# Attention logits of a two-layer trunk: one float32 product, or three float32r products of high and low parts

## The chip, the core and the metric

The kernel runs on one core of a Trainium2 chip. The metric is the device time of one execution in microseconds (us). Data passes between the engines of the core by semaphores: TensorE (PE, matmuls and transposes into PSUM), VectorE (DVE), ScalarE (ACT), GpSimd (POOL) and SyncE (SP, which here issues DMAs). Each engine works through its own instructions in order.

## The reference

The input is 512 tokens of 1024 features. Layer 0 is a Mamba-2 mixer and a convolutional feed-forward block (FFN). Then keys and values are projected once from the stream, and layer 1 is a differential attention over them and a second FFN. The change is in the attention, which is, cut to what matters:

```python
q = rms_norm((rms_norm(x, ln_g) @ q_w).reshape(b, s, 8, 2, 64), q_norm_g)   # k alike
logits = einsum('bqhcd,bkhcd->bhcqk', qblk, k) * 64 ** -0.5 + bias
p = softmax(where(dist >= 0, logits, -inf))
attn = p[:, :, 0] - lam * p[:, :, 1]
o = einsum('bhqk,bkhd->bqhd', attn, v)
```

There are 8 heads. Each has two maps c, each with a query and a key vector of 64 elements; the two softmax maps are subtracted with a learned weight, and the difference is applied to one value vector of 128 elements. The result of each head is normalised and goes through the output projection. Everything is float32.

## The kernel before

The kernel keeps the stream transposed: `xT` is 8 tiles of 128 features by 512 tokens. Large matmuls aren't done in float32. Both operands are split into a high part, rounded to float32r, and a low part, the float32r difference, and `mm3` (lines 174 to 177) adds three float32r products: high by high, high by low, low by high. Weights are loaded in an order fixed by `plan` (lines 68 to 116), two chunks ahead of their use, by SP (line 138), and split on arrival by ScalarE (lines 144, 148) and VectorE (lines 145, 149).

The attention begins at line 761. `proj` (line 783) makes 512 columns of a projection for all tokens: four chunks of weights, and for each 24 float32r matmuls 512 columns wide into four PSUM banks (lines 791 to 793), 96 in all. `qk` (line 805) does that for the keys or queries of four heads (k0 and q0 are heads 0 to 3, k1 and q1 heads 4 to 7). Its evacuation scales each 128 tokens by ScalarE (line 811), squares (812) and sums by VectorE (813). After an inverse square root (`rsqrt_act`, line 336) VectorE normalises (820), TensorE transposes (824), and ScalarE copies to SBUF with the gain (825). The tiles `kT[i]` and `qT[i]` (lines 779, 780) are [128, 4, 512], float32: the 128 rows of a head are map 0 on rows 0 to 63 and map 1 on rows 64 to 127. `vproj` (829) does the values.

A head is three units (`Unit`, line 837): query blocks 0 and 1 together, block 2, and block 3, of 128 queries each, which see 128, 256, 384 and 512 keys. A unit goes through four steps. `logits` (847): for each block and each map, one float32 matmul of 64 rows (line 867), in PSUM bank m for map m; VectorE adds the bias and takes the maximum (870); ScalarE does the exponentials with their sums (878). `weigh` (881): the reciprocal and the subtraction of the maps (883 to 888). `turn` (891): transposes (896) and a copy by ScalarE (897). `values` (899): float32 matmuls with the values (905) and a copy (908). After the last unit of a head `finish` (911) normalises its output, transposes it (921) and splits it (924, 925). The bias of a head is loaded as a Toeplitz tile `tr` from a small table in DRAM (852) and reversed by VectorE (853).

`heads` (929) staggers the steps of successive units. `weave` (368) puts pieces of other work between them: with heads 0 to 3 stand the projections k1, q1 and v1, with heads 4 to 7 the output projection of heads 0 to 3 (`attn_out`, line 952, 96 matmuls); the output projection of heads 4 to 7 comes last. On top of that a scheduler sets the final order of each engine's instructions, and moves some of them past others. The buffers come from pools: of a tag with n buffers, the tile after n others reuses the first, once that is no longer read.

```python
for m in range(2):
    rows = slice(64 * m, 64 * (m + 1))
    pe.matmul(pss[m][:, c], qT[i2][rows, h4, i * P:(i + 1) * P], kT[i2][rows, h4, :n],
              start=True, stop=True)
```

Of the kernel before, what the change touches and what calls it, by code (L numbers as in the profile page):

```python
# [9 lines left out]
F32 = mybir.dt.float32  # L10
F32R = mybir.dt.float32r
I32 = mybir.dt.int32
AF = mybir.ActivationFunctionType
ALU = mybir.AluOpType
# [4 lines left out]
P = 128  # L19
T = 512  # L20
D = 1024
KB = D // P
NT = T // P
# [8 lines left out]
AH = 8  # L32
# [7 lines left out]
def trunk_kernel(ctx: ExitStack, tc, x, ssm_ln_g, ssm_in_w, ssm_conv_w, ssm_conv_b, ssm_dt_bias,  # L40
# [62 lines left out]
    def tok_plan(key, w, c0, gcol):  # L103
        for k in range(0, KB, 2):
            plan.append(("%s_%d" % (key, k), *w_cols(w, k, 2, c0, 512), gcol + k))
# [2 lines left out]
    tok_plan("q0", q_w[0], 0, 40)  # L108
    tok_plan("v0", kv_w, D, 32)
    tok_plan("k1", kv_w, 512, 32)  # L110
    tok_plan("q1", q_w[0], 512, 40)
    tok_plan("v1", kv_w, D + 512, 32)
    for i in range(2):
        for c in range(4):
            plan.append(("ao%d_%d" % (i, c), *w_cols(attn_out_w[0], 4 * i, 4, c * 256, 256)))
# [84 lines left out]
    c2 = cp.tile([P, 80], F32, name="c2")  # L200
# [16 lines left out]
    with tc.tile_pool(name="ph0", bufs=1) as p0:  # L217
# [43 lines left out]
        ps = aux_bank("pst")  # L261
# [74 lines left out]
    def rsqrt_act(v, pl, name, shape, n):  # L336

        m = pl.tile(shape, F32, tag="rs_m", name="rsm_" + name, bufs=2)
        t = pl.tile(shape, F32, tag="rs_t", name="rst_" + name, bufs=2)
        dve.tensor_scalar(out=m, in0=v, scalar1=1.0 / n, scalar2=EPS, op0=ALU.mult, op1=ALU.add)  # L340
        act.activation(v, m, AF.Ln)
        act.activation(v, v, AF.Exp, scale=-0.5)
        dve.tensor_tensor(out=t, in0=v, in1=v, op=ALU.mult)
        dve.scalar_tensor_tensor(out=t, in0=t, scalar=-0.5, in1=m, op0=ALU.mult, op1=ALU.mult)
        dve.scalar_tensor_tensor(out=v, in0=t, scalar=1.5, in1=v, op0=ALU.add, op1=ALU.mult)
# [18 lines left out]
    def run(gen):  # L364
        for _ in gen:
            pass
# [11 lines left out]
    def chain(*gens):  # L378
        for g in gens:
            yield from g  # L380
# [380 lines left out]
    with tc.tile_pool(name="att_o", bufs=1) as op_, tc.tile_pool(name="att", bufs=1) as ap:  # L761
# [5 lines left out]
        hb = NBIAS // 2  # L767
        for i in range(2):
            oh = ap.tile([32, hb], F32, tag="p0", name="oh%d" % i, bufs=3)
            bv = ap.tile([AH, hb], F32, tag="p1", name="bv%d" % i, bufs=3)  # L770
            sync.dma_start(oh, onehot[:, i * hb:(i + 1) * hb])
            ps = aux_bank("ps_rb%d" % i)
            pe.matmul(ps[:AH, :hb], rb, oh, start=True, stop=True)
            act.activation(bv, ps[:AH, :hb], AF.Copy)
            if i == 0:
                dve.memset(bv[:, 0:P - 1], NEG)
            sync.dma_start(bd[:, i * hb:(i + 1) * hb], bv)

        kT = [ap.tile([P, 4, T], F32, name="kT%d" % i) for i in range(2)]
        qT = [ap.tile([P, 4, T], F32, name="qT%d" % i) for i in range(2)]  # L780
        vt = [ap.tile([P, D], F32, name="vt%d" % b) for b in range(NT)]

        def proj(key, evac):
# [19 lines left out]
            yield  # L803

        def qk(key, dst, gcol):
            kn, ss = [], ap.tile([P, NT, 8], F32, tag="qss", name="ss" + key, bufs=2)

            def evac(b, ps, rt):
                t = ap.tile([P, T], F32, tag="kn", name="kn%s_%d" % (key, b), bufs=4)
                s = ap.tile([P, T], F32, tag="ksq", name="ksq%s_%d" % (key, b), bufs=1)  # L810
                act.activation(t, ps, AF.Copy, scale=rt[:, 2 * b:2 * b + 1])
                act.activation(s, t, AF.Square)
                dve.reduce_sum(ss[:, b, :], s.rearrange("p (a q) -> p a q", a=8), axis=AX.X)
                kn.append(t)

            yield from proj(key, evac)
            rsqrt_act(ss, ap, key, [P, NT, 8], 64)
            for b in range(NT):
                v = kn[b].rearrange("p (a q) -> p a q", a=8)
                dve.tensor_tensor(out=v, in0=v, in1=ss[:, b, :].unsqueeze(2).to_broadcast([P, 8, 64]),  # L820
                                  op=ALU.mult)
                ps = aux_bank("kt%s_%d" % (key, b))
                for h in range(4):
                    pe.transpose(ps[:, h * P:(h + 1) * P], kn[b][:, h * P:(h + 1) * P], ident)
                act.activation(dst[:, :, b * P:(b + 1) * P], ps.rearrange("p (h t) -> p h t", h=4),
                               AF.Copy, scale=c2[:, gcol:gcol + 1])
            yield

        def vproj(key, i):
            def evac(b, ps, rt):  # L830
                act.activation(vt[b][:, i * 512:(i + 1) * 512], ps, AF.Copy, scale=rt[:, 2 * b:2 * b + 1])
            yield from proj(key, evac)
# [4 lines left out]
        class Unit:  # L837
# [9 lines left out]
            def logits(self):  # L847
                h, tag, st = self.h, self.tag, self.st
                if self.part == 0:
                    st["tb"] = ap.tile([P, T], F32, tag="tb", name="tb%d" % h, bufs=2)  # L850
                    tr = ap.tile([P, T], F32, tag="tr", name="tr%d" % h, bufs=1)
                    sync.dma_start(tr, bass.AP(tensor=bd.tensor, offset=h * NBIAS, ap=[[1, P], [1, T]]))
                    dve.tensor_copy(st["tb"], tr[:, ::-1])
                    st["ot"] = ap.tile([P, NT, P], F32, tag="ot", name="ot%d" % h, bufs=2)
                i2, h4 = h // 4, h % 4
                k = len(self.ii)
                mx = ap.tile([P, k, 2], F32, tag="mx%d" % k, name="mx" + tag, bufs=3)
                self.sm = ap.tile([P, k, 2], F32, tag="sm%d" % k, name="sm" + tag, bufs=3)
                self.p = [ap.tile([P, T], F32, tag="p%d" % m, name="lg%s_%d" % (tag, m), bufs=3)
                          for m in range(2)]  # L860
                pss = [aux_bank("lg%s_%d" % (tag, m)) for m in range(2)]
                for j, i in enumerate(self.ii):
                    n = (i + 1) * P
                    c = slice(self.off[j], self.off[j] + n)
                    for m in range(2):
                        rows = slice(64 * m, 64 * (m + 1))
                        pe.matmul(pss[m][:, c], qT[i2][rows, h4, i * P:(i + 1) * P], kT[i2][rows, h4, :n],
                                  start=True, stop=True)
                    for m in range(2):
                        dve.tensor_tensor_reduce(self.p[m][:, c], pss[m][:, c],  # L870
                                                 st["tb"][:, (3 - i) * P:], 1.0, -3.0e38,
                                                 ALU.add, ALU.max, mx[:, j, m:m + 1])
                dve.tensor_scalar(out=mx, in0=mx, scalar1=-1.0, scalar2=None, op0=ALU.mult)
                for j, i in enumerate(self.ii):
                    n = (i + 1) * P
                    for m in range(2):
                        v = self.p[m][:, self.off[j]:self.off[j] + n]
                        act.activation(v, v, AF.Exp, bias=mx[:, j, m:m + 1],
                                       accum_out=self.sm[:, j, m:m + 1])
# [30 lines left out]

        def finish(h, st):
            ot = st["ot"]
            sq = ap.tile([P, T], F32, tag="ksq", name="osq%d" % h, bufs=1)
            so = ap.tile([P, NT], F32, tag="so", name="so%d" % h, bufs=2)
            act.activation(sq, fl(ot), AF.Square)
            dve.reduce_sum(so, sq.rearrange("p (a q) -> p a q", a=NT), axis=AX.X)
            rsqrt_act(so, ap, "o%d" % h, [P, NT], P)
            dve.tensor_tensor(out=ot, in0=ot, in1=so.unsqueeze(2).to_broadcast([P, NT, P]), op=ALU.mult)
            ps = aux_bank("oT%d" % h)
            for i in range(NT):  # L920
                pe.transpose(ps[:, i * P:(i + 1) * P], ot[:, i, :], ident)
            oh_ = op_.tile([P, T], F32R, tag="oh", name="oh%d" % h, bufs=6)
            ol_ = op_.tile([P, T], F32R, tag="ol", name="ol%d" % h, bufs=6)
            act.activation(oh_, ps, AF.Copy, scale=c2[:, 50:51])
            dve.scalar_tensor_tensor(out=ol_, in0=ps, scalar=c2[:, 50:51], in1=oh_.bitcast(F32),
                                     op0=ALU.mult, op1=ALU.subtract)
            return oh_, ol_
# [24 lines left out]
        def attn_out(i, os, norm):  # L952
            for c in range(4):
# [7 lines left out]
                    add_to_stream(m, ps, 24, norm)  # L961
                    yield

        run(qk("k0", kT[0], 48))
        run(qk("q0", qT[0], 49))
        run(vproj("v0", 0))
        os0, os1 = [], []
        weave(heads(range(0, 4), os0),
              chain(qk("k1", kT[1], 48), qk("q1", qT[1], 49), vproj("v1", 1)), 2, 5)
        weave(heads(range(4, 8), os1), attn_out(0, os0, None), 1, 6)  # L970
        run(attn_out(1, os1, norm1))

# [37 lines left out]
```

## Time and profile before

| what | us |
|---|---|
| median of 3 runs (lowest, highest) | 1390.85 (1390.69, 1392.38) |
| the profiled execution's own time | 1389.46 |
| its span, first to last instruction | 1387.6 |
| TensorE busy | 1367.3 |
| VectorE busy | 893.6 |
| ScalarE busy | 671.5 |
| the first logits matmul starts at | 833.4 |
| the last head's transposes start at | 998.8 |

The profile is of one execution. Its views used below are the page (busy time of each engine, the span in 40 slices, the chain that ended last); the busy time of each engine in chosen stretches, where the number behind x counts instructions; the timeline of an engine (start and duration in us, line, operation, output <- inputs, shape, and how many records in a row are drawn together); the chain of work that ended last, piece by piece in order of time; and the groups of instructions by line and shape (busy us, mean ns, idle before). TensorE's matmuls are pipelined, so a record is longer than its share of the engine: what a matmul costs in a row of them is read from one start to the next. A float32 matmul leaves two records.

### The profile page before, as it was taken

To read this page: it belongs to the slowest core of one execution; us is meant where nothing else is said; L and a number is where in the kernel's file an instruction comes from. 1 tells how busy PE (TensorE), PEld (TensorE's weight loads), DVE (VectorE), ACT (ScalarE), POOL (GpSimd) and SP (SyncE) were. 2 spreads that over 40 slices of the span, in tenths; PEclk is the share of its full clock that TensorE was granted. 3 is DMA by queue.
4 is the path that set the end of the run, shared out by engine and by line. 5 is a ranking of instruction groups with operands and counts; after the bars stand their busy time and mean duration, and the time that the engine had idled before them with its cause. 6 is when DMAs were issued, how large, how long until landed. Compare 5 with 4: busy or idle time off the path is not lost.

```text
span 1387.6 us, 17001 instructions
## 1 busy us (share of the span) xinstructions
PE 1367.3 (99%) x6480; PEld 1105.0 (80%) x6480; DVE 893.6 (64%) x1481; ACT 671.5 (48%) x1108; POOL 93.2 (7%) x117
## 2 busy tenths in 40 slices
PE   8999999999999999999999999999999999999998
PEld 6777787787878888888888786786778888888886
DVE  6687767768677775357754546748687774367741
ACT  6785644742344443134433557757654442144431
POOL 4330300300020000000001000000020000000000
PEclk9999999999999999999999999999999999999999
DMA  6655433432223333233323422221133332333322
GB/s 183 163 148 148 129 91 107 129 103 65 80 88 107 91 97 101 91 104 95 93 82 112 114 90 68 66 87 39 48 103 93 93 105 91 99 99 91 99 92 69
DMA packets 188422, 137.18 MB, mean 99 GB/s; under 512 B 6852, under 2 KB 177268, under 8 KB 188340
## 3 DMA queue, kind: packets, MB, share of 16 engines
q1 hardware_dynamic: 181312, 122.93, 30.1%
q0 software_dynamic: 4400, 12.01, 2.9%
q10 hardware_dynamic: 2628, 1.15, 0.3%
q8 instruction: 51, 0.84, 0.2%
q14 instruction: 31, 0.25, 0.1%
HBM read 133.82 MB, written 2.25 MB: 98 GB/s over the span
## 4 chain that ended last, share of the span: by engine, by line
PE 76%; DVE 5%; ACT 4%; issue 1%; DMA 0%; POOL 0%; POOLq 0%; ACTq 0%
PE ps_u L175 6%; PE ps_u L177 6%; PE ps_d L176 6%; PE ps_d L177 6%; PE ps_u L176 6%; PE ps_d L175 6%; PE ps_g L176 6%; PE ps_g L177 6%; PE ps_g L175 5%; PE ps_in L175 2%; PE ps_in L177 2%; PE ps_in L176 2%; PE ps_o L176 2%; PE ps_o L177 2%; PE ps_o L175 1%
## 5 line engine op out<-in xcount | busy, mean ns | idle before, releaser
L176 PE MATMUL ps_g<-xgl,wh_g 128*128 128x512 f32 x352 | 137.2, 390 | 1.5 <-DVE xgl L319 1.5
L175 PE MATMUL ps_d<-hh,wh_d 128*128 128x512 f32 x352 | 137.5, 391 | 0.0
L177 PE MATMUL ps_d<-hh,wl_d 128*128 128x512 f32 x352 | 137.2, 390 | 0.0
L175 PE MATMUL ps_u<-xgh,wh_u 128*128 128x512 f32 x352 | 137.1, 390 | 0.0
L176 PE MATMUL ps_u<-xgl,wh_u 128*128 128x512 f32 x352 | 137.1, 390 | 0.0
L175 PE MATMUL ps_g<-xgh,wh_g 128*128 128x512 f32 x352 | 137.0, 389 | 0.1
L176 PE MATMUL ps_d<-hl,wh_d 128*128 128x512 f32 x352 | 137.0, 389 | 0.0
L177 PE MATMUL ps_u<-xgh,wl_u 128*128 128x512 f32 x352 | 136.9, 389 | 0.0
L177 PE MATMUL ps_g<-xgh,wl_g 128*128 128x512 f32 x352 | 136.9, 389 | 0.0
L175 PE MATMUL ps_in<-xgh,wh_in 128*128 128x512 f32 x320 | 126.9, 397 | 0.0
L177 PE MATMUL ps_in<-xgh,wl_in 128*128 128x512 f32 x320 | 126.3, 395 | 0.0
L176 PE MATMUL ps_in<-xgl,wh_in 128*128 128x512 f32 x320 | 125.9, 393 | 0.0
L149 DVE TENSOR_TENSOR wl_d<-wr_d,wh_d 128x1024 fp32r<-128x1024 f32 (+1 forms) x48 | 54.5, 1136 | 91.7 <-ACT wh_d L148 91.5
L148 ACT ACTIVATE wh_d<-wr_d 128x1024 fp32r<-128x1024 f32 (+1 forms) x48 | 47.5, 990 | 129.5 <-PE ps_d L176 115.3
L724 ACT ACTIVATE hh<-vg 128x512 fp32r<-128x512 f32 x44 | 27.8, 631 | 114.9 <-DVE vg L723 114.9
L707 DVE TENSOR_TENSOR uu<-ps_u,nr_f 128x512 f32<-128x512 f32 x44 | 30.4, 692 | 79.6 <-PE ps_u L177 79.6
L176 PEld LDWEIGHTS ps_g<-xgl,wh_g 128*128 128x128 f32 x352 | 66.1, 188 | 16.0 <-DVE xgl L319 2.3
L175 PEld LDWEIGHTS ps_g<-xgh,wh_g 128*128 128x128 f32 x352 | 66.1, 188 | 14.2 <-ACT xgh L318 0.5
L177 PEld LDWEIGHTS ps_u<-xgh,wl_u 128*128 128x128 f32 x352 | 66.1, 188 | 13.7
L176 PEld LDWEIGHTS ps_u<-xgl,wh_u 128*128 128x128 f32 x352 | 66.1, 188 | 13.7
L176 PEld LDWEIGHTS ps_d<-hl,wh_d 128*128 128x128 f32 x352 | 66.1, 188 | 13.6
L177 PEld LDWEIGHTS ps_d<-hh,wl_d 128*128 128x128 f32 x352 | 66.1, 188 | 13.5
(315 smaller groups left out, 2950.4 us busy)
## 6 DMA issues: line engine op xcount, KB each, us to landing
wr_g<-in_ffn_up_w_dram SPq DMA_DIRECT2D x44, 512.0 KB, 3.8
wr_u<-in_ffn_up_w_dram SPq DMA_DIRECT2D x44, 512.0 KB, 3.9
wr_in<-in_ssm_in_w_dram SPq DMA_DIRECT2D x40, 512.0 KB, 3.9
wr_d<-in_ffn_down_w_dram SPq DMA_DIRECT2D x40, 512.0 KB, 3.5
m<-cumd POOLq DMA_DIRECT2D x16, 512.0 KB, 5.1
wr_out<-in_ssm_out_w_dram SPq DMA_DIRECT2D x16, 512.0 KB, 3.4
wr_k<-in_kv_w_dram SPq DMA_DIRECT2D x8, 512.0 KB, 3.9
wr_q<-in_q_w_dram SPq DMA_DIRECT2D x8, 512.0 KB, 4.1
```

Source lines behind the costliest of these rows:

```text
L148: act.activation(wh[:, :n], raw[:, :n], AF.Copy)
L149: dve.tensor_tensor(out=wl[:, :n], in0=raw[:, :n], in1=wh[:, :n].bitcast(F32), op=ALU.subtract)
L175: pe.matmul(ps, wh, xh, start=start, stop=False)
L176: pe.matmul(ps, wh, xl, start=False, stop=False)
L177: pe.matmul(ps, wl, xh, start=False, stop=stop)
L707: dve.tensor_tensor(out=u, in0=ps, in1=r, op=ALU.mult)
L724: act.activation(h, ga, AF.Copy)
```

## The change

The transposed keys and queries are stored as a high and a low float32r part, in tiles of two heads ([128, 2, 512]) in place of four: ScalarE copies with the gain to the high part, VectorE computes the low part from the same PSUM bank. The tiles come from rings, three buffers for keys and two for queries (each for high and low). The logits of a block are three float32r products (high by high, high by low, low by high), each for both maps in turn, map 0 on rows 0 to 63 and map 1 on rows 64 to 127; they add up in PSUM. To make room, map 1 of the logits (`p1`) has two buffers for three, the squares `ksq` and `osq` and the bias tile `tr` go to tiles of the pool `bp` that the norms also use (`tr` then has two buffers), and `qss` has one buffer for two. The projection v1 moves ahead of q1, in the weights' plan and in the code.

```diff
-    tok_plan("q1", q_w[0], 512, 40)
     tok_plan("v1", kv_w, D + 512, 32)
+    tok_plan("q1", q_w[0], 512, 40)
...
-            bv = ap.tile([AH, hb], F32, tag="p1", name="bv%d" % i, bufs=3)
+            bv = ap.tile([AH, hb], F32, tag="p1", name="bv%d" % i, bufs=2)
...
-        kT = [ap.tile([P, 4, T], F32, name="kT%d" % i) for i in range(2)]
-        qT = [ap.tile([P, 4, T], F32, name="qT%d" % i) for i in range(2)]
+        kT, qT = [], []
...
-            kn, ss = [], ap.tile([P, NT, 8], F32, tag="qss", name="ss" + key, bufs=2)
+            kn, ss = [], ap.tile([P, NT, 8], F32, tag="qss", name="ss" + key, bufs=1)
...
-                s = ap.tile([P, T], F32, tag="ksq", name="ksq%s_%d" % (key, b), bufs=1)
+                s = bp.tile([P, T], F32, tag="nr", name="ksq%s_%d" % (key, b))
...
+            new = []
+            for q in range(2):
+                new.append([ap.tile([P, 2, T], F32R, tag=key[0] + hl, name="%s%s_%d" % (key, hl, q),
+                                    bufs=3 if key[0] == "k" else 2) for hl in "hl"])
+            dst += new
+            g = c2[:, gcol:gcol + 1]
...
-                act.activation(dst[:, :, b * P:(b + 1) * P], ps.rearrange("p (h t) -> p h t", h=4),
-                               AF.Copy, scale=c2[:, gcol:gcol + 1])
+                for q in range(2):
+                    src = ps[:, q * 256:(q + 1) * 256].rearrange("p (h t) -> p h t", h=2)
+                    h_, l_ = (a[:, :, b * P:(b + 1) * P] for a in new[q])
+                    act.activation(h_, src, AF.Copy, scale=g)
+                    dve.scalar_tensor_tensor(out=l_, in0=src, scalar=g, in1=h_.bitcast(F32),
+                                             op0=ALU.mult, op1=ALU.subtract)
...
-                    tr = ap.tile([P, T], F32, tag="tr", name="tr%d" % h, bufs=1)
+                    tr = bp.tile([P, T], F32, tag="nsq", name="tr%d" % h, bufs=2)
...
-                i2, h4 = h // 4, h % 4
+                (qh, ql), (kh, kl), h2 = qT[h // 2], kT[h // 2], h % 2
...
-                self.p = [ap.tile([P, T], F32, tag="p%d" % m, name="lg%s_%d" % (tag, m), bufs=3)
+                self.p = [ap.tile([P, T], F32, tag="p%d" % m, name="lg%s_%d" % (tag, m), bufs=3 - m)
...
-                    for m in range(2):
-                        rows = slice(64 * m, 64 * (m + 1))
-                        pe.matmul(pss[m][:, c], qT[i2][rows, h4, i * P:(i + 1) * P], kT[i2][rows, h4, :n],
-                                  start=True, stop=True)
+                    for s, (a, b) in enumerate(((qh, kh), (qh, kl), (ql, kh))):
+                        for m in range(2):
+                            rows = slice(64 * m, 64 * (m + 1))
+                            pe.matmul(pss[m][:, c], a[rows, h2, i * P:(i + 1) * P], b[rows, h2, :n],
+                                      start=s == 0, stop=s == 2)
...
-            sq = ap.tile([P, T], F32, tag="ksq", name="osq%d" % h, bufs=1)
+            sq = bp.tile([P, T], F32, tag="nr", name="osq%d" % h)
...
-        run(qk("k0", kT[0], 48))
-        run(qk("q0", qT[0], 49))
+        run(qk("k0", kT, 48))
+        run(qk("q0", qT, 49))
...
-              chain(qk("k1", kT[1], 48), qk("q1", qT[1], 49), vproj("v1", 1)), 2, 5)
+              chain(qk("k1", kT, 48), vproj("v1", 1), qk("q1", qT, 49)), 2, 5)
```

More of the change, by code (lines that the diff above doesn't have):

```diff
@@ L110, in trunk_kernel @@
     tok_plan("k1", kv_w, 512, 32)
+    tok_plan("v1", kv_w, D + 512, 32)
     tok_plan("q1", q_w[0], 512, 40)
-    tok_plan("v1", kv_w, D + 512, 32)
     for i in range(2):
```

## Prediction

> **What bounds the kernel now.** I read the page first, then the engines by stretch, then TensorE's rows in order of time, and last the chain that ended last. The page:
>
> ```profile
> span 1387.6 us, 17001 instructions
> ...
> PE 1367.3 (99%) x6480; PEld 1105.0 (80%) x6480; DVE 893.6 (64%) x1481; ACT 671.5 (48%) x1108; POOL 93.2 (7%) x117
> ...
> PEclk9999999999999999999999999999999999999999
> ...
> PE 76%; DVE 5%; ACT 4%; issue 1%; DMA 0%; POOL 0%; POOLq 0%; ACTq 0%
> ```
>
> TensorE (PE) is busy 99% of the span, at the full granted clock, and holds 76% of the chain. So the time is TensorE's work plus the short gaps in it. The change lies in attention, which is these stretches, from the view of busy times by stretch: heads 0 to 3 with the k1 and q1 projections beside them, the rest of q1 and v1 alone, and heads 4 to 7 with the output projection beside them.
>
> ```profile
> core 0: us, PE busy (x) PEld busy (x) DVE busy (x) ACT busy (x) POOL busy (x), PEclk, DMA share, GB/s
> 833.40:902.30 68.90, 66.92 (x357) 49.50 (x357) 49.60 (x166) 53.87 (x142) 0.00 (x0) 1.00 0.24 66
> 902.30:936.80 34.50, 34.35 (x167) 27.86 (x166) 15.78 (x28) 18.34 (x33) 0.00 (x0) 1.00 0.26 84
> ...
> 936.80:1000.20 63.40, 61.26 (x325) 43.73 (x324) 47.07 (x158) 46.13 (x126) 0.00 (x0) 1.00 0.15 47
> ```
>
> TensorE is nearly full, but VectorE (DVE) and ScalarE (ACT) are at 47.1 and 46.1 of 63.4 us in the last stretch: there is little slack when TensorE has less to do meanwhile. What the logits cost is read from TensorE's timeline (start, duration, and the number of records run together); L867 is the logits.
>
> ```profile
> 883.79 0.49 PE L867 MATMUL lg<-kT,qT 64*128 64x128 f32 x4
> 884.21 0.55 PE L896 MATMUL at<-ident,lg 128*128 128x128 f32 x3
> ...
> 884.91 0.70 PE L867 MATMUL lg<-kT,qT 64*128 64x256 f32 x4
> 885.55 0.94 PE L905 MATMUL po<-vt,at 128*128 128x128 f32 x6
> ...
> 886.85 0.92 PE L867 MATMUL lg<-kT,qT 64*128 64x384 f32 x4
> 887.70 0.66 PE L896 MATMUL at<-ident,lg 128*128 128x128 f32 x4
> ...
> 891.26 0.39 PE L792 MATMUL ps_q<-wl_q,xgh 128*128 128x512 f32 x1
> 891.48 0.39 PE L793 MATMUL ps_q<-wh_q,xgl 128*128 128x512 f32 x1
> 891.80 1.13 PE L867 MATMUL lg<-kT,qT 64*128 64x512 f32 x4
> 892.86 0.55 PE L896 MATMUL at<-ident,lg 128*128 128x128 f32 x3
> ```
>
> From a group's start to the next start, the pair of maps takes 0.42, 0.64, 0.85 and 1.06 us at 128, 256, 384 and 512 keys: 0.21 us fixed and 0.213 per 128 keys. Each map is one float32 matmul of two records. A float32 record on all 128 rows takes 0.67 / 6 = 0.11 us per 128 columns (the row at 902.29 below), so two maps one after the other would take 4 x 0.11 = 0.44 per 128 keys. They take 0.213: **the two maps run side by side already**. Beside that, a group is entered at a price: 0.32 us from the last ps_q start to the logits, against 0.22 between the two ps_q starts, so 0.1 us.
>
> **The change part by part: the logits on TensorE.** A float32 matmul of a pair becomes three float32r matmuls each. Their rate is in the warm-up, in the groups by form, and in the chain, where one 512-wide float32r matmul (ps_ao, ps_q) stands at 0.23 us:
>
> ```profile
> L260 PE MATMUL warm<-wmv,wst 128*128 128x512 f32 x6 | 1.6, 407 | 0.0
> L260 PE MATMUL warm<-wmv,wst 128*128 128x256 f32 x6 | 0.9, 282 | 0.0
> L260 PE MATMUL warm<-wmv,wst 128*128 128x128 f32 x6 | 0.8, 267 | 0.0
> ```
>
> Six in a row are busy 1.6, 0.9 and 0.8 us; less the last one's own time, divided by five, that is 0.24, 0.12 and 0.11 us apart (I use the chain's 0.228 for 512). At 128 columns nothing is gained over 256. With both maps side by side as now, three steps cost 0.33, 0.36, 0.52 (0.173 each, between its neighbours) and 0.68 us against 0.213, 0.427, 0.64 and 0.853: +0.12, -0.07, -0.12, -0.17, in sum -0.24 per head, **-1.9 us** over 8 heads. That is all that the fewer passes can give.
>
> Three things eat at it. First, the fixed 0.21 us: it is either what the change of the array's mode costs, once per group, or two open weight loads of 0.105, one per float32 record; then three products pay three, +0.105 x 4 x 8 = +3.4 us. The rows don't decide, so 0 to 3.4; I take the middle, **+1.7**.
>
> Two rules of the Trainium skill pull apart here. "TensorE: Matmul & The Clock Gate", Part 3, says that a weight load overlaps matmuls in flight only when their row group differs, and its section on LDWEIGHTS gives 128 / 1.2 GHz for 128 columns, by my estimate 107 ns, which agrees with the 0.105 above; by that rule it is the whole 3.4 and the sum 1.7 us higher. "TensorEngine Tiling (Array Packing)", Key Properties, says that a change of the tiling mode drains TensorE; by that alone the fixed part is paid once per group, as now, and the sum is 1.7 us lower.
>
> Second, order. As a scheduler puts the changed program's instructions, not all groups alternate the maps. That this costs is shown before: the first group holds eight matmuls of mixed widths.
>
> ```profile
> 833.36 3.29 PE L867 MATMUL lg<-kT,qT 64*128 64x128 f32 x16
> 836.58 0.50 PE L791 MATMUL ps_k<-wh_k,xgh 128*128 128x512 f32 x1
> ```
>
> It takes 3.22 us to the next start, where four separate groups take 2.97 and one group should save three fixed parts. So a matmul whose half is taken holds up those behind it. In the built order eight groups stand as map 0, 0, 1, 1, 0, 1: four steps for three, five times at 256 (0.12), once at 384 (0.17), twice at 128 (0.11), 1.0 us. Heads 6 and 7 have map 0 and map 1 of the 256 keys apart (2 x 0.36), head 4 its 384 and 512 (some 1.0): together 2.7 us. Before pays for such orders too, some 2.1 us by the same count (the eight-matmul groups, the lone maps of heads 1 and 5, head 7). And there are 32 groups for 28, at some 0.18 us for entering and leaving: 0.7. Net **+1.3**. So the logits come out at -1.9 + 1.7 + 1.3 = +1.1 us.
>
> **Evacuation.** Each 128 tokens of a projection now need two 256-wide ScalarE copies and two VectorE subtractions in place of one 512-wide copy.
>
> ```profile
> L825 ACT ACTIVATE kT<-ktk,c 128x512 f32<-128x512 f32 x8 | 5.2, 687 | 1.4 <-PE ktk L824 1.4
> L825 ACT ACTIVATE qT<-ktq,c 128x512 f32<-128x512 f32 x8 | 5.0, 683 | 0.1
> ...
> L887 ACT ACTIVATE lg<-lg,sm 128x256 f32<-128x256 f32 x8 | 4.0, 495 | 0.0
> L888 DVE SCALAR_TENSOR_TENSOR lg<-lg,sm,lg 128x256 f32<-128x256 f32 x8 | 3.8, 481 | 0.2
> ```
>
> 32 x 0.48 = 15.4 us more on VectorE, 32 x 0.495 - 16 x 0.685 = 4.9 us more on ScalarE. For k0 and q0 the v0 projection covers it; k1's quarter falls into the first stretch (VectorE 49.6 + 3.9 of 68.9 us). I cost that at +0.5; with its cover gone it would be the 3.9.
>
> **q1 last.** Before, v1's 96 matmuls hide the way from q1's projection to its transposes:
>
> ```profile
> 902.29 0.67 PE po L905 x6
> ...
> 908.03 0.70 ACT knq L811
> ...
> 917.94 0.70 DVE knq L820
> 918.78 1.17 PE ktq L824 x8
> ```
>
> This takes 10.8 us from the first evacuation, which starts three quarters of a chunk, 18 x 0.228 = 4.1 us, before the projection ends: 6.7 remain. In the built order 27 matmuls of the output projection stand there, 6.2 us, and ten more ahead of the logits, so I cost the chain itself at 0; without them 6.7. But those matmuls, 35 until the logits begin, are missing later, beside heads 4 to 7: 35 x 0.228 = 8.0 us of cover. What is late next is the end of the pipeline:
>
> ```profile
> 993.89 1.10 PE po L905 x8
> ...
> 998.81 0.63 PE oT L921 x4
> ...
> 1000.14 1.05 PE ps_ao L175 x4
> ```
>
> From the last values (end 994.99) to the last head's transposes are 3.8 us, hidden by 16 matmuls. In the built order 11 (2.5 us) are left there, and none between the transposes and the copy that the projection waits for: 1.3 idle, 0.7 more, and the previous head's chain is no longer covered: **+2**. At the start of the pipeline TensorE already waits (idle in brackets):
>
> ```profile
> 841.07 0.33 PE L896 MATMUL at<-ident,lg 128*128 128x128 f32 x1 [0.57 <-DVE lg L888]
> ```
>
> There the first logits end some 1.0 us sooner, 14 projection matmuls stand for 16, and the softmax chain gains some 0.5 only: **+1**. Two buffers for map 1 of the logits (p1) cost nothing by themselves: in VectorE's order the weighing of a unit stands ahead of the unit after next in any case. The bias tiles (tr), now two, load earlier on SP's queue; behind them stand weight loads, two chunks ahead of use. The k and q rings are free when refilled, since heads 0 and 1, or 0 to 3, are over: 0, and up to a chunk's load if not.
>
> **Sum:** 1.1 + 0.5 + 0 + 2 + 1 = +4.6 us. The profiled execution took 1389.46 us (span 1387.6 and 1.9 around it), so 1394.1; it lies 1.4 us under the median of the runs, 1390.85, so I state 1395.5.
>
> **Rivals.** *Maps one after the other.* If float32r matmuls on half the rows don't run side by side, a group has six steps: 0.66, 0.72, 1.04, 1.37 against 0.21, 0.43, 0.64, 0.85, which is +1.66 per head, 13.3 us. With 0.7 for the groups and some 1 for waits: +15, 1405.9. For it: no row shows float32r on 64 rows. Against: float32 does it. 0.10.
>
> *VectorE and ScalarE become the bound beside heads 4 to 7.* If that stretch stays 63.4 us with 8.0 us less on TensorE, all 8.0 are lost in place of the 2: +10.6, 1401.5. For it: 47 and 46 us of work in in-order queues with a chain per unit. Against: 16 us of slack. 0.10.
>
> *The gain holds and waits don't grow.* If the halves take their matmuls independently of the order and loads stay hidden, before's 2.1 us of bad order go too: -1.9 - 2.1 + 0.7 = -3.3, 1387.6. It decides by whether pairs at 512 keys take 0.68 + 0.21 and no more gaps come after 936. 0.13.
>
> *A wash.* Loads stay hidden (0 for 1.7) and the waits come to about 2: near +1, 1392. 0.22.
>
> **How the numbers follow.** The forecast, +2.8 to +9 us, has 0.45. About 0.2%, 2.8 us, is what a measurement of this kernel can tell from no change. Slower: 0.45 + 0.10 + 0.10 = 0.65; same 0.22; faster 0.13. The range goes from 1388.5 to 1406: it takes in the wash, the busy engines and nearly all of the maps in turn, and leaves out most of the gain that holds.
>
> **What would show it.** The logits of 512 keys at three steps of 0.23 plus 0.21 to 0.32 us in a group that alternates confirm the rates; 1.6 means maps in turn. Groups in the order 0, 0, 1, 1, 0, 1 should be one step longer. The gap ahead of the first transposes of the weights (841 us) should grow from 0.6 to some 1.5 us, and a gap of 1 to 2 us appear ahead of the last oT. It is wrong if the stretch from the first logits to the last oT is shorter than its 165.4 us, or if attention's VectorE rows hold back TensorE in the middle of heads 0 to 3.

## The result, and the profile after

The changed kernel takes 1401.62 us, median of 4 runs (1399.51 to 1405.41); the kernel before, run beside it, 1390.77 us (1389.08 to 1392.38). The ratio is 1.0083, 95% interval 1.0064 to 1.0103: **slower by 10.85 us** where 4.6 were forecast. The profiled execution of the changed kernel is one of the four, and the longest: 1405.41 us, span 1403.5, 15.9 us over the span of before's. The page of its profile, the lines that answer to those of before (engines' busy time, then the chain that ended last):

```profile
span 1403.5 us, 17176 instructions
...
PE 1375.6 (98%) x6544; PEld 1117.1 (80%) x6544; DVE 902.1 (64%) x1513; ACT 676.0 (48%) x1124; POOL 94.0 (7%) x117
...
PE 78%; DVE 5%; ACT 3%; issue 1%; DMA 1%; POOL 0%; ACTq 0%; DVEq 0%; POOLq 0%
```

TensorE is busy 8.3 us more in a span that is 15.9 us longer, so about half of the loss is time in which it stands still. Busy times by stretch (columns as before: stretch, its length, busy time and instructions of PE, PEld, DVE, ACT and POOL, granted clock, DMA) show where. The stretches are heads 0 to 3, the rest of the projections, the way from q1's last matmul to the first logits of head 4, and heads 4 to 7:

```profile
836.50:905.40 68.90, 66.72 (x386) 51.56 (x386) 51.89 (x172) 54.41 (x145) 0.00 (x0) 1.00 0.20 62
905.40:937.40 32.00, 31.80 (x152) 26.03 (x151) 12.62 (x21) 15.28 (x26) 0.00 (x0) 1.00 0.31 99
937.40:947.80 10.40, 10.18 (x53) 8.06 (x51) 8.20 (x17) 6.90 (x14) 0.00 (x0) 1.00 0.16 53
947.80:1011.60 63.80, 57.77 (x331) 43.80 (x330) 46.61 (x161) 44.64 (x124) 0.00 (x0) 0.97 0.11 34
```

The first three are nearly full, and nothing is lost there: from the first logits to the transposes of head 3 it is 77.2 us, before 78.3. The last one is as long as before's 63.4 us, though 23 matmuls of the output projection fewer stand in it; TensorE is busy 57.8 us of it, before 61.3, and its granted clock is below one.

From TensorE's timelines I take the times of the same events in both kernels (in us from the span's start; the last column is how much later the changed kernel is):

| event | before | after | later by |
|---|---|---|---|
| first logits | 833.36 | 836.46 | 3.1 |
| first logits of head 4 | 936.80 | 947.82 | 11.0 |
| transposes of the last head (oT7) | 998.81 | 1010.16 | 11.3 |
| last matmul of the output projection | 1015.54 | 1026.67 | 11.1 |
| first ps_u of FFN1 | 1023.83 | 1037.25 | 13.4 |
| last matmul of FFN1 | 1381.37 | 1397.30 | 15.9 |

The 3.1 us ahead of the attention are none of the change's: TensorE ran at half clock there for 10.2 us (at 15.5 and 175.9 us), before for 3.4 us, which makes (10.2 - 3.4) / 2 = 3.4 us. After 998 us half clock came three more times, in before not at all until the end. The stretches are cut at its edges; the number behind POOL's is the granted clock:

```profile
998.00:1001.90 3.90, 1.31 (x10) 1.13 (x11) 3.02 (x8) 2.15 (x6) 0.00 (x0) 1.00 0.00 0
1001.90:1005.30 3.40, 3.40 (x16) 3.30 (x17) 0.75 (x1) 1.56 (x3) 0.00 (x0) 0.50 0.00 0
1005.30:1012.20 6.90, 4.81 (x27) 3.71 (x26) 2.68 (x7) 2.01 (x5) 0.00 (x0) 0.99 0.00 0
1012.20:1015.60 3.40, 3.40 (x10) 2.63 (x9) 1.50 (x4) 1.13 (x2) 0.00 (x0) 0.50 0.00 0
...
1036.10:1042.90 6.80, 6.80 (x20) 5.59 (x20) 3.23 (x14) 0.80 (x1) 0.00 (x0) 0.50 0.26 77
```

Each stretch at half clock follows one in which TensorE stood still for a while: 1.3 of 3.9 us busy, 4.8 of 6.9. They cost half their length, 6.8 us in this execution. To see past them I use, for each run, its time less (1 - granted clock) x span: the time that it would have had at full clock, if TensorE bound it throughout. By that the changed kernel has a median of 1392.7 and 9.1 us lost to the clock (4 runs), the kernel before 1386.2 and 4.2 (17 runs of the first set of experiments). So of the 10.85 us **about 6.5 are time at full clock, and about 4.9 are clock**. These two are good to a microsecond or so: the clock is listed to 0.001, which is 1.4 us, and in the four sets of runs the kernel before has 1384.7 to 1387.2 us at full clock and loses 2.8 to 4.2.

### The profile page after: what moved, and what is told of

The parts are those of the page before. It is cut to its first block, busy times and chain, and to the rows that moved or that the text cites. A ratio compares the mean times of both kernels' runs of the same rounds, so it can differ in the third digit from the quotient of the medians.

```text
span 1403.5 us, 17176 instructions
## 1 busy us (share of the span) xinstructions
PE 1375.6 (98%) x6544; PEld 1117.1 (80%) x6544; DVE 902.1 (64%) x1513; ACT 676.0 (48%) x1124; POOL 94.0 (7%) x117
## 4 chain that ended last, share of the span: by engine, by line
PE 78%; DVE 5%; ACT 3%; issue 1%; DMA 1%; POOL 0%; ACTq 0%; DVEq 0%; POOLq 0%
PE ps_u L175 6%; PE ps_u L176 6%; PE ps_u L177 6%; PE ps_d L175 6%; PE ps_d L176 6%; PE ps_d L177 6%; PE ps_g L176 6%; PE ps_g L177 6%; PE ps_g L175 6%; PE ps_in L175 2%; PE ps_in L177 2%; PE ps_in L176 2%; PE ps_o L176 2%; PE ps_o L177 2%; PE ps_o L175 2%; PE lg L877 1%
## 5 line engine op out<-in xcount | busy, mean ns | idle before, releaser
L175 PEld LDWEIGHTS ps_u<-xgh,wh_u 128*128 128x128 f32 x352 | 66.8, 190 | 13.9
L177 PEld LDWEIGHTS ps_g<-xgh,wl_g 128*128 128x128 f32 x352 | 66.1, 188 | 13.7
```

Of the source, the lines that this page charges most:

```text
L175: pe.matmul(ps, wh, xh, start=start, stop=False)
L177: pe.matmul(ps, wl, xh, start=False, stop=stop)
```

## The experiments

The theory after the result: the order, v1 ahead of q1, is the cause. 35 matmuls of the output projection now cover q1's chain and are missing beside heads 4 to 7, and the idle spots that come of it let the clock halve. Rivals: the split itself (three products, two evacuations, rings, shared buffers) costs it; the halvings are chance. All ratios are to the kernel before in the same set of runs; 0.001 is 1.4 us.

**1. The order or the split.** e1_order_alone is the kernel before with only the order changed:

```diff
-    tok_plan("q1", q_w[0], 512, 40)
     tok_plan("v1", kv_w, D + 512, 32)
+    tok_plan("q1", q_w[0], 512, 40)
...
-              chain(qk("k1", kT[1], 48), qk("q1", qT[1], 49), vproj("v1", 1)), 2, 5)
+              chain(qk("k1", kT[1], 48), vproj("v1", 1), qk("q1", qT[1], 49)), 2, 5)
```

> The kernel before, with one edit: the value projection v1 ahead of the query projection q1, in the plan of the weights and in the chain beside heads 0 to 3. Logits stay float32, queries and keys stay in their full tiles. Theory (the order is the cause: the matmuls of attn_out that cover q1's chain are missing beside heads 4 to 7, whose length VectorE and ScalarE set, and the idle spots at the end of attention let TensorE's clock halve): +7 to +10 us over the kernel before, some 1398 to 1401, with idle spots of 1.5 us or more ahead of the last two transposes of oT. Rival (the three products, the split of queries and keys and the shared buffers cost it): 0 to +2 us, 1391 to 1393.

e2_split_alone is the changed kernel with the same two edits undone:

```diff
-    tok_plan("v1", kv_w, D + 512, 32)
     tok_plan("q1", q_w[0], 512, 40)
+    tok_plan("v1", kv_w, D + 512, 32)
...
-              chain(qk("k1", kT, 48), vproj("v1", 1), qk("q1", qT, 49)), 2, 5)
+              chain(qk("k1", kT, 48), qk("q1", qT, 49), vproj("v1", 1)), 2, 5)
```

> The changed kernel with q1 ahead of v1 again, as in the kernel before: three products, split queries and keys, rings and shared buffers all stay. Theory (the order is the cause): 0 to +2 us against the kernel before, 1390.5 to 1393, first logits to the transposes of the last head 165 to 167 us, no halving of the clock after 990 us. Rival (the split and the rings are the cause): +8 to +11 us, 1399 to 1402.

Measured: the order alone 1401.61 us, ratio 1.0068 (1.0050 to 1.0087); the split alone 1389.34 us, ratio 0.9990 (0.9976 to 1.0005). **The order is the whole loss**, as far as these intervals tell, and the split costs nothing that can be measured. By the ratios e1 is 9.5 us over the kernel before, as its theory had it, and e2 1.4 us under, a little below the 0 to +2 of the theory. At full clock the order alone is 6.1 us over before's 1386.2 and the split alone 1.6 us under it. In the trace of the split alone no half clock follows 176 us until the end, and heads 4 to 7 are full (columns as above):

```profile
939.90:1001.20 61.30, 59.94 (x351) 45.11 (x350) 46.76 (x158) 46.10 (x126) 0.00 (x0) 1.00 0.15 44
```

VectorE and ScalarE work 46.8 and 46.1 us here and 46.6 and 44.6 in the changed kernel; TensorE is busy 59.9 us here, and 57.8 us in the changed kernel, whose stretch is 2.5 us longer.

**2. Is that stretch set by VectorE and ScalarE, whatever TensorE does?** Three of the eight blocks of the first attn_out are computed twice, once for nothing, in the changed kernel (e6) and with the split alone (e8):

```diff
-                    ps = mm_bank("ps_ao%d_%d" % (i, m))
-                    for k in range(4):
-                        mm3(ps, wh[:, k, j * P:(j + 1) * P], wl[:, k, j * P:(j + 1) * P],
-                            os[k][0], os[k][1], k == 0, k == 3)
+                    for r in range(2 if i == 0 and m > 4 else 1):
+                        ps = mm_bank("ps_ao%d_%d_%d" % (i, m, r))
+                        for k in range(4):
+                            mm3(ps, wh[:, k, j * P:(j + 1) * P], wl[:, k, j * P:(j + 1) * P],
+                                os[k][0], os[k][1], k == 0, k == 3)
```

> The changed kernel with three of the eight blocks of the first half of attn_out computed twice, the first time into a bank that nobody reads: 36 more matmuls of 0.228 us, 8.2 us of TensorE, placed beside heads 4 to 7, where the changed kernel has 35 fewer than the kernel before. Theory (the stretch from the first logits of head 4 to the last oT is set by VectorE and ScalarE): the stretch grows by 0 to 2 us and the time is 1400.5 to 1404. Rival (TensorE's length counts): +8 us, 1408 to 1411.

> The run with q1 ahead of v1 and the logits split, with the same 36 matmuls more (8.2 us of TensorE) beside heads 4 to 7. Theory (with the old order TensorE is already full there, and what does not fit goes behind the last head): +6 to +8.5 us over the run with the split alone, 1395.5 to 1398. Rival (the stretch has room there too): 0 to +2 us, 1389.5 to 1391.5.

Measured: e6 1405.71 us, ratio 1.0115 (1.0097 to 1.0132), so 0.0032 or 4.4 us over the changed kernel's 1.0083; e8 1396.65 us, ratio 1.0046 (1.0029 to 1.0062), 7.8 us over the split alone. e8 came as the theory had it. e6 did not: neither 0 to 2 nor 8. The stretch from head 4's first logits to oT7 grew from 60.6 us (62.3 less 1.7 of half clock) to 66.2, by 5.6 of the 8.2 us. **That theory falls in this form**: TensorE's length does count beside heads 4 to 7, and only some 2.6 us of idle time could be filled. Where they lie, the steps from one head's transposes to the next show, with the matmuls of the output projection in each (n, counted in TensorE's timeline) taken off at 0.228 us apiece:

| step | before: us, n, rest | split alone | after | after with 36 more (e6) |
|---|---|---|---|---|
| head 4's logits to oT4 | 26.25, 46, 15.8 | 29.23, 57, 16.2 | 28.64, 52, 16.8 | 32.28, 69, 16.5 |
| oT4 to oT5 | 15.08, 28, 8.7 | 12.59, 18, 8.5 | 13.57, 21, 8.8 | 14.85, 28, 8.5 |
| oT5 to oT6 | 13.79, 29, 7.2 | 11.26, 22, 6.2 | 11.77, 12, 9.0 | 12.19, 24, 6.7 |
| oT6 to oT7 | 6.90, 17, 3.0 | 6.89, 17, 3.0 | 8.36, 12, 5.6 | 6.92, 12, 4.2 |
| behind oT7 | n 72 | n 78 | n 60 | n 60 |

The rest is alike in the first two steps. It grows in the last two of the changed kernel, where only 12 matmuls each are left: by 2.8 us from oT5 to oT6 and by 0.9 (without the half clock) from oT6 to oT7, against the split alone. The engines have room; it is the chains of the last two heads that lie open. TensorE's rows (start, duration, line, output and inputs, records, idle before in brackets):

```profile
998.38 0.55 PE L906 MATMUL at<-ident,lg 128*128 128x128 f32 x3 [0.42 <-DVE lg L898]
998.76 0.83 PE L915 MATMUL po<-vt,at 128*128 128x128 f32 x6
1001.80 1.03 PE L931 MATMUL oT<-ident,ot 128*128 128x128 f32 x4 [2.21 <-DVE ot L928]
...
1008.46 0.39 PE L177 MATMUL ps_ao<-oh,wl_ao 128*128 128x512 f32 x1
1010.16 0.63 PE L931 MATMUL oT<-ident,ot 128*128 128x128 f32 x4 [1.31 <-DVE ot L928]
1011.57 1.58 PE L175 MATMUL ps_ao<-oh,wh_ao 128*128 128x512 f32 x4 [0.78 <-ACT oh L934]
```

and the same places in the kernel before, which has 0.18 us of idle time there:

```profile
991.92 0.63 PE L921 MATMUL oT<-ident,ot 128*128 128x128 f32 x4
...
998.81 0.63 PE L921 MATMUL oT<-ident,ot 128*128 128x128 f32 x4 [0.18 <-DVE ot L918]
999.20 0.48 PE L175 MATMUL ps_ao<-oh,wh_ao 128*128 128x512 f32 x1
```

In the changed kernel it is 2.2 us ahead of oT6, 1.3 ahead of oT7 and 0.8 behind it. The prediction named all three. It priced the last two, at 1.3 and 0.7 us, and they came so; the first, which it gave no price, is more than both.

**3. Do the idle spots set off the half clock?** e3_filled_gaps puts 20 transposes for nothing into each of the two spots:

```diff
             dve.reduce_sum(so, sq.rearrange("p (a q) -> p a q", a=NT), axis=AX.X)
+            if h in (6, 7):
+                fill = aux_bank("fill%d" % h)
+                for t in [ot[:, i % 4, :] for i in range(8)] + [sq[:, (i % 4) * P:(i % 4 + 1) * P] for i in range(12)]:
+                    pe.transpose(fill[:, :P], t, ident)
             rsqrt_act(so, ap, "o%d" % h, [P, NT], P)
```

> The changed kernel with 20 more transposes for each of heads 6 and 7, of what finish holds at that moment, into a PSUM bank that nobody reads; they stand in the idle spots of 2.5 and 1.7 us ahead of the transposes of oT. Theory of the clock (the idle spots set off the halvings at 1002 and 1012 us): those two halvings are gone, and the time falls by 2 to 4 us against the changed kernel, to 1398 to 1400, though more work is done. Rival (the halvings come by themselves, or from the whole load before them): they stay, and the time is the same or up to 1 us more, 1401 to 1403.

Measured: 1402.73 us, ratio 1.0081 (1.0063 to 1.0098), the time of the changed kernel. Yet the two halvings are gone from its trace (same columns as the stretches above):

```profile
996.00:1002.00 6.00, 5.72 (x47) 5.25 (x48) 3.57 (x9) 3.34 (x9) 0.00 (x0) 1.00 0.00 0
1002.00:1009.00 7.00, 6.68 (x44) 5.39 (x44) 2.78 (x7) 2.01 (x5) 0.00 (x0) 1.00 0.00 0
```

The halvings went from the trace and the gain did not come. The transposes pushed six matmuls of the output projection behind the last head (66 there for 60, 1.4 us), at full clock the median is 1.5 us longer, and by the medians of all executions, of which the trace is one, the clock gives back only 0.7 us. One halving stays: at 1030.2 us, for 6.8 us, behind the idle spot at the start of FFN1. Over the traces of all runs here, with spots measured from one matmul's start to the next: a spot of 2.5 to 3.0 us ahead of oT6 was followed by half clock in three of four traces (after, e1 and e9, not e4), one of 1.7 with one of 1.05 behind it, at oT7, in three of five (after, e4 and e9, not e1 and e6); with the spots filled or absent it never came there.

What tells these apart is how the spot lies in time. Within each trace all edges of half clock lie on one grid with a step of 3.413 us: in the changed kernel it begins at 1001.93, 1012.17 and 1036.07 us, 3 and 7 steps apart. Take in each of the 14 traces, from 20 us to the end of FFN1, the stretches between one edge of its grid and the next that run at full clock. All 13 in which TensorE stood idle for 1.75 us or more were followed by half clock, 15 of 32 with 1.0 to 1.75 us, and one of some 5480 with less. In after, e1 and e9 the whole spot ahead of oT6, 2.2 to 2.6 us idle, lies in one stretch; in e4 an edge at 998.0 us halves it. At oT7 it is closer: 2.1, 2.0 and 1.7 us idle in one stretch were followed by half clock, 1.7 and 1.5 us were not.

**4. The start of FFN1.** In the changed kernel the first ps_g (FFN1's first products) waits there, on the last two xgl (the low parts of the scaled stream, which VectorE computes); the second fence has VectorE and GpSimd in the same microseconds:

```profile
1030.98 0.49 PE L175 MATMUL ps_g<-xgh,wh_g 128*128 128x512 f32 x1
1033.62 0.50 PE L176 MATMUL ps_g<-xgl,wh_g 128*128 128x512 f32 x1 [2.15 <-DVE xgl L319]
...
1035.31 0.50 PE L176 MATMUL ps_g<-xgl,wh_g 128*128 128x512 f32 x1 [0.72 <-DVE xgl L319]
```

```profile
1030.69 1.21 DVE L149 TENSOR_TENSOR wl_g<-wr_g,wh_g 128x1024 fp32r<-128x1024 f32 x1
1031.82 3.43 DVE L319 SCALAR_TENSOR_TENSOR xgl<-xT,c,xgh 128x512 fp32r<-128x512 f32 x2
...
1031.59 3.12 POOL L395 TENSOR_TENSOR nacc_f<-nacc_f,nsq_f 128x512 f32<-128x512 f32 x2 [2.58 <-ACT nsq_f L394]
```

Two xgl take 3.43 us beside GpSimd's two sums for the norm. In the kernel before, the last one took 0.74 us, and GpSimd's sum began 0.36 us later than it:

```profile
1020.99 0.74 DVE L319 SCALAR_TENSOR_TENSOR xgl<-xT,c,xgh 128x512 fp32r<-128x512 f32 x1
...
1021.35 1.51 POOL L395 TENSOR_TENSOR nacc_f<-nacc_f,nsq_f 128x512 f32<-128x512 f32 x1 [2.57 <-ACT nsq_f L394]
```

"SBUF — State Buffer" of the Trainium skill, Summary: rules for kernel authors, says that a VectorE instruction with two SBUF inputs and a GpSimd one that reads SBUF exclude each other, the second to issue waiting until the first is over; the trace agrees, in that GpSimd's sum issued first (1031.59) and 0.74 became 1.7. e9_norm_on_vector takes the last four sums off GpSimd:

```diff
-            pool.tensor_tensor(out=self.acc, in0=self.acc, in1=sq, op=ALU.add)
+            eng = dve if self.name == "f1" and k >= 4 else pool
+            eng.tensor_tensor(out=self.acc, in0=self.acc, in1=sq, op=ALU.add)
```

> The changed kernel with the last four of the seven sums of squares for FFN1's norm on VectorE instead of GpSimd. Theory (at the start of FFN1 two xgl take 3.4 to 3.5 us beside GpSimd's sum and 0.75 us each without it; the shorter stretch behind the last head leaves TensorE waiting for the last of them, and the idle spot of 2.6 us sets off the halving of the clock): the spot falls under 1.3 us, no halving follows it, and the time falls by 2 to 5 us, to 1396.5 to 1399.5. Rival (the adds to the stream and the weight splits ahead of xgl make the spot, or VectorE is now late by its sums): 1400.5 to 1403.

Measured: 1397.23 us, ratio 1.0056 (1.0038 to 1.0074), 3.8 us under the changed kernel by the ratios. The last xgl now stand at

```profile
1025.82 0.74 DVE L319 SCALAR_TENSOR_TENSOR xgl<-xT,c,xgh 128x512 fp32r<-128x512 f32 x1
1026.48 0.68 DVE L396 TENSOR_TENSOR nacc_f<-nacc_f,nsq_f 128x512 f32<-128x512 f32 x1
1027.08 0.74 DVE L319 SCALAR_TENSOR_TENSOR xgl<-xT,c,xgh 128x512 fp32r<-128x512 f32 x1
```

and from the last matmul of the output projection to the first ps_u it is 6.5 us, for 10.6 in the changed kernel and 8.3 before. No half clock follows 1012 us until the end. The theory holds: no spot over 1.2 us is left there. Why the changed kernel reaches this place worse than before is read from the traces, and no run tests it by itself: with only 60 matmuls left behind the last head its last four adds to the stream run in two pairs on VectorE, and each pair of xgl behind them meets a pair of sums; in the kernel before, with 72 left, the last two adds run apart. A spot of 2.5 to 2.7 us here was followed by half clock in all six traces that have one (after, e1, e3, e4, e5, e6); with shorter spots or none in one of the other eight.

**5. The order of the maps.** Holding each group to map 0, map 1 in turn, in the changed kernel (e4) and with the split alone (e5):

```diff
-                            pe.matmul(pss[m][:, c], a[rows, h2, i * P:(i + 1) * P], b[rows, h2, :n],
-                                      start=s == 0, stop=s == 2)
+                            mm = pe.matmul(pss[m][:, c], a[rows, h2, i * P:(i + 1) * P], b[rows, h2, :n],
+                                           start=s == 0, stop=s == 2)
+                            if s or m:
+                                tc.keep_in_program_order(mm)
```

> The changed kernel with the six matmuls of each group of logits held to the order of the program, map 0 and map 1 in turn, so that no group runs 0,0,1,1,0,1 or 0,0,0 and 1,1,1. Theory (heads 4 to 7 are bound by VectorE and ScalarE): the groups sum to 24.5 to 25.5 us instead of 26.6, and of this at most 0.5 us reaches the end, 1401 to 1402. Rival (TensorE's own length still counts beside heads 4 to 7): all of 1.5 to 2 us is gained, 1399.5 to 1400.

> The run with q1 ahead of v1 and the logits split, with the six matmuls of each group of logits held in the order map 0, map 1 in turn. First theory (with the old order TensorE's own length counts in the attention): 1 to 2 us under the run with the split alone, 1387 to 1388.5, and the groups sum to 24.5 to 25.5 us. Rival (chains of VectorE and ScalarE set the length there too): no difference, 1389 to 1390.

Measured: e4 1401.92 us, ratio 1.0083 (1.0063 to 1.0103): the groups sum to 25.3 us for 26.6, as expected, and none of it reaches the end. e5 1395.78 us, ratio 1.0047 (1.0031 to 1.0063): the groups sum to 25.0 us for 26.0, and **the time is 7.9 us longer** than with the split alone, which neither theory had. The trace says where: the held order moved the output projection, 131 of its matmuls stand beside heads 4 to 7 (114 with the split alone) and 61 behind the last head (78). The stretch grew by 3.2 us, the output projection still ended 78.1 us behind head 4's first logits as with the split alone, and then FFN1's start waits as in the changed kernel, with 10.2 us of half clock behind it:

```profile
1021.27 0.51 PE L175 MATMUL ps_g<-xgh,wh_g 128*128 128x512 f32 x1 [0.46 <-ACT xgh L318]
1023.92 0.80 PE L176 MATMUL ps_g<-xgl,wh_g 128*128 128x512 f32 x1 [2.15 <-DVE xgl L319]
1024.51 0.63 PE L177 MATMUL ps_g<-xgh,wl_g 128*128 128x512 f32 x1
```

e11_alternate_norm is e5 with the sums on VectorE, to see whether that is all of it:

> The run with q1 ahead of v1 and the maps held in turn of each group (which came out 5.7 us over the kernel before), with the same four sums on VectorE. Theory (what that run lost, it lost at the start of FFN1: 2.65 us idle and a halving of 10.2 us right behind it): 4 to 8 us less, 1388 to 1392. Rival (it lost beside heads 4 to 7, by the order of the queues): 0 to 2 us less, 1393.5 to 1396.

Measured: 1388.44 us, ratio 0.9994 (0.9983 to 1.0005), 7.4 us under e5, so nearly all of it comes back. But the same sums take 1.9 us off the split alone too (e10 below). Against that run, with the sums on VectorE in both, e11 is 2.5 us longer by the ratios, which is hardly clear of noise.

e7_maps_in_turn has the loops over m and s exchanged with the split alone, and the six held in that order: the three products of map 0, then those of map 1:

```diff
-                    for s, (a, b) in enumerate(((qh, kh), (qh, kl), (ql, kh))):
-                        for m in range(2):
-                            rows = slice(64 * m, 64 * (m + 1))
+                    for m in range(2):
+                        rows = slice(64 * m, 64 * (m + 1))
+                        for s, (a, b) in enumerate(((qh, kh), (qh, kl), (ql, kh))):
```

> The run with q1 ahead of v1 and the logits split, with the three products of map 0 held ahead of the three of map 1 in every group, so that no two maps stand side by side. Theory (two matmuls on the two row halves run at once): a group of 512 keys takes 6 steps of 0.23 us, some 1.4 to 1.6 us instead of 0.9, all 32 groups 9 to 14 us more, of which most reaches the end: 1396 to 1404. Rival (only TensorE's queue order differs, the halves do not overlap; or the chains of VectorE and ScalarE hide it): 1388.5 to 1391.

Measured: 1396.37 us, ratio 1.0055 (1.0035 to 1.0076), 9.0 us over the split alone, so at first sight as the theory had it. The groups tell otherwise: in sum 29.6 us for 26.0, 3.6 us more and not 9 to 14, and most groups keep their length. TensorE's rows of one group of 384 keys:

```profile
894.92 0.45 PE L877 MATMUL lg<-k0h,q0h 64*128 64x384 f32 x2
895.20 0.34 PE L877 MATMUL lg<-k0l,q0h 64*128 64x384 f32 x2
895.38 0.34 PE L877 MATMUL lg<-k0h,q0l 64*128 64x384 f32 x2
895.65 0.44 PE L908 MATMUL at<-ident,lg 128*128 128x128 f32 x2
```

Two records start together at each step, 0.73 us from first to next, as in a group that alternates. So the two halves ran side by side although the queue held three products of one map first. The rest of the 9.0 us is clock: at full clock e7 is 3.7 us over the split alone, and 5.6 us more are lost to the clock, with a halving of 6.8 us at 862.6 behind an idle spot of 1.5 us.

**6. The sums on VectorE with the old order.** The split alone with the four sums on VectorE:

> The run with q1 ahead of v1 and the logits split, with the same four sums on VectorE. First theory: its idle spot of 1.26 us at the start of FFN1 falls to some 0.5 us, 0.5 to 1.5 us under the run with the split alone, 1388 to 1389, which would be under both kernels. Rival: the same time, 1389 to 1390.

And the kernel before with the sums alone:

> The kernel before, with nothing but the last four sums of squares for FFN1's norm on VectorE, to part what the split and what the sums give in the run that had both. Theory (the split gives 1 to 2 us by itself, as the run with the split alone has it): 0.5 to 1.5 us under the kernel before, so 1 to 2 us over the run with split and sums. Rival (the sums give it all): 2.5 to 3.5 us under the kernel before, the time of that run.

Measured: e10 1386.89 us, ratio 0.9976 (0.9960 to 0.9992), under the kernel before by 3.3 us and under the changed kernel by 14.9 us, by the ratios. e12 1386.47 us, ratio 0.9984 (0.9967 to 1.0000). e10 is 1.9 us under the split alone, somewhat more than forecast. e12 is 2.2 us under the kernel before, between its theory and its rival. By the ratios two thirds of e10's gain are the sums'; whether the split adds the 1 us that stands between the two, their intervals leave open.

## Why the prediction was right in sign and too small

The kernel is slower, as forecast, and the time lies in the stated range. But 10.85 us is beyond the forecast's own +2.8 to +9: the range holds it because it had been drawn wide enough for two rivals, neither of which happened, so this is in part luck. Term by term:

- **Passes, -1.9: right, and the loads cost nothing.** A group that alternates, in the changed kernel:

```profile
967.23 0.50 PE L877 MATMUL lg<-k1h,q1h 64*128 64x512 f32 x2
967.57 0.39 PE L877 MATMUL lg<-k1l,q1h 64*128 64x512 f32 x2
967.80 0.40 PE L877 MATMUL lg<-k1h,q1l 64*128 64x512 f32 x2
968.12 0.55 PE L906 MATMUL at<-ident,lg 128*128 128x128 f32 x3
```

  Three steps of 0.23 and a fixed 0.2: 0.89 us, with 0.48, 0.56 and 0.72 at 128, 256 and 384 keys. The fixed part is paid once per group, so the open weight loads were 0 and not +1.7: the lower of the prediction's two readings.
- **Order of maps and groups, +1.3: too small, about +3.** The groups sum to 26.6 us for 26.0 before, +0.6 in place of the forecast +1.1; as the groups that alternate save 2.5 us, the orders and entries lose 3.1. The first group, of 24 matmuls, took 3.83 us, 0.7 of it idle on VectorE's maxima. The prediction's reason, that a matmul whose half is taken holds up those behind it, isn't what the rows show. Five groups of six matmuls run clearly longer than one that alternates (at 845.91, 864.98, 888.70, 961.45 and 979.30 us; the fourth, of 384 keys, 1.02 us for 0.72). In all five the second map starts 0.10 to 0.31 us behind the first, and the semaphore of VectorE or ScalarE that it waits for came 0.04 us before that, in the third 0.14 us: it waited for them. And e7's groups, with three products of one map first in the queue, mostly kept their length. And little of it counts: e4 took 1.3 us off these groups and the time stayed.
- **Evacuation +0.5 and the ramp +1: about 0.** From the first logits to head 4's it is 111.4 us for 103.4, and the 35 matmuls of the output projection that now stand in it are 8.0. The gap ahead of the first transposes of the weights fell from 0.96 to 0.37 us, start to start, where growth was forecast.
- **q1's chain, 0: right.** The stretch from 937.4 to 947.8 us above is full, 10.2 of 10.4.
- **"What is late next is the end of the pipeline ... +2": this step failed.** It priced what lies open behind the last head's values, and that came as priced: 1.3 us idle ahead of the last oT, 0.8 behind it. The previous head's chain stands in the sum at nothing, and the start of FFN1 not at all. But the 35 matmuls cost 8.0 us ahead of head 4, and should have come back but for 2. At full clock 1.4 us came back in heads 4 to 7, 1.9 behind the last head, and 1.7 of that went again at the start of FFN1: some 1.6 in all, and 6.4 lost. The missing cover opened oT6's chain (2.2 us idle), and behind the shorter work after the last head the adds, splits and norm sums of the stream lay open, which no step had.
- **The clock was left out.** The page's full tenths for before were taken as given. But the idle spots that the change opens are followed by half clock, and this is the rest of the loss, about 4.9 us.
- **The rival of the busy VectorE and ScalarE** came within 0.2 us of the time, and its mechanism is not what happened: both engines were busy 73% and 70% of that stretch, and 36 matmuls more cost 5.6 of their 8.2 us. It is the forecast's own mechanism, the latency of the last heads, at three times its price, and the clock. The rival of the maps one after the other is refuted by the rows, even for a program that orders them so.

## What to carry to other kernels

Work that fills a wait early is taken from where it would fill a wait later: before moving a step, count the filler of each later chain, and price the last ones to run, not only the very last. An idle spot of 2 us on TensorE cost about twice that or more here where half clock followed, which added 1.7, 3.4 or 5.1 us. And where the work at the end of a stage gets shorter, look at what the other engines still do there: here one order of the logits cost 7.9 us with four sums on GpSimd, and 2.5 us, hardly clear of noise, with these on VectorE.

## What the runs showed of the hardware that was not expected

- Half clock comes in stretches of 3.4, 6.8 and 10.2 us, whole multiples of 3.4, and follows idle spots of TensorE. "TensorE: Matmul & The Clock Gate" of the Trainium skill, Part 1, has a free-running window of 3413 ns, which agrees; its section Why this matters for your kernels warns of idle gaps above some 3 us, and here nine of ten spots of 2.5 to 3.0 us, start to start, were enough. What told them apart was the idle time within one stretch of the grid: 1.75 us or more was followed by half clock each time.
- Float32r matmuls on the two row halves started within 0.01 us of each other although the three of one map stood ahead of the other's in the built order (e7). The same page, Part 3, says that matmuls start strictly in program order; these rows differ. So for the two row halves it does not hold that an engine works through its own instructions in order.
- An xgl on VectorE takes 0.74 us alone and 1.7 us beside GpSimd's sum; four sums moved, and the start of FFN1 is 4.1 us shorter in the trace (10.6 to 6.5).
